# Seven seven-product pairs instead of eight in the gated MLP's up projection, with three plain pairs at its end

## The chip, the cores and the metric

The kernel runs on one NeuronCore of a Trainium2 chip. The core has five engines that work beside each other, each through its own instructions in order: TensorE (PE in the profile; its weight loads are PEld), VectorE (DVE), ScalarE (ACT), GpSimd (POOL) and SyncE (SP, which here only issues transfers). ACT issues transfers too (ACTq in the rows). The metric is the device time of one execution in microseconds (us): the median of three runs before is 1050.01 us (1048.56 to 1051.01).

## The reference, cut to what matters

One layer of an encoder over 512 tokens of width 1024 in float32: four token mixers, a cross-attention into 256 memory tokens, and a gated MLP with a causal depthwise convolution. The change lies in the MLP:

```python
hf = _rms_norm(x, norm_ffn_pre[l])
u = _dwconv_causal(hf @ w_up[l], ffn_dw[l]) + ffn_dw_b[l]      # 1024 -> 2 x 2816, width 3
u_g, u_v = jnp.split(u, 2, axis=-1)
yff = (jax.nn.silu(u_g) * u_v) @ w_down[l]                     # 2816 -> 1024
x = x + _rms_norm(yff, norm_ffn_post[l])
```

## The kernel before, in words

**Numbers.** A float32 matrix is held as two parts: a high part (a cast on ACT, `wh`, `hth`, `tokh`) and a low part (the value less its high part, on DVE, `wl`, `htl`, `tokl`). A product is three matmuls: high by high, and each high by the other's low (`mm3`, which ends in L244).

**Up projection (`up_jobs`).** The 5632 columns of `w_up` are 22 gate blocks and 22 value blocks of 128 columns; pair j is gate block j with value block j. A block's result is channels by tokens (128 x 512) in a PSUM bank, summed over 8 row tiles. A *plain* block takes 8 x 3 matmuls with 512 moving columns (`plain`, `channel_major`), so a plain pair takes 48. A *seven-product* pair (`seven`) takes both blocks as a 2 x 2 matrix (upper and lower half of the 1024 rows, gate and value) by a 2 x 2 matrix of `hf` (upper and lower half of the channels, first and second 256 tokens), and does seven products instead of eight in Winograd's form: 7 x 4 x 3 = 84 matmuls with 256 moving columns. It needs sums of its weights (four GpSimd additions in `load_a`, on the raw tiles `wq`, into `sums` and `s`), three additions of products (on DVE, with the copies `mu` on ACT), and four sums of tokens, which all seven-product pairs share: `token_sums` builds them in the last four `qa` tiles, and `token_split` splits them into `tokh` and `tokl`. Of a pair that is done, `done` adds the bias, convolves (`taps`, L624), and leaves silu(gate) times value in half of a `qa` tile; `qa` tile q holds pairs 2q and 2q + 1.

Before, pairs 0 to 4 are plain, then eight times a seven-product pair (5, 7, ... 19) is interleaved with the plain pair behind it (6, 8, ... 20), and pair 21 is plain.

**Down projection (`down_jobs`).** It runs Winograd's form over token halves, column halves of `w_down` and the two pairs in a `qa` tile, in two phases over q = 0 to 10. Phase 0 makes products M1, M6, M5, M7 into all eight PSUM banks. Its weights come in two tiles `dw` for each q, of parts of `w_down` and of weight sums that went through DRAM: class `Sums` loads two tiles `wp` (ACT queue, L568), adds (L572 to L575) and stores (L579), one q at a time, in the loop over the up pairs. The buffers of `wp` serve the third and fourth `dw` tile later, the two of `wq` the first and second. The activations of q must be summed first: `down_sums(q)`, three GpSimd additions of 128 x 256 (L1665 to L1667), the last of which writes into the `qa` tile. Room for the sums (`down_places`): the tile `z7` for q = 0 and 1, `tokh` for q = 2 to 9 and `tokl` for q = 10, which come free only when the last seven-product pair has read them. `activations(phase, q)` then splits `qa` and `pairs`: for q = 0 into the two `wr` tiles, for q = 1 to 4 into quarters of the tiles of `hf` (`hth`, `htl`), which come free when the last up block has been multiplied.

**Order.** `run_blocks` fetches the weights of three jobs ahead of the one it multiplies. The program is then put in order by a scheduler that goes by a modelled time, within the dependences; `issue_after` adds an order against one instruction. The order on each engine is fixed in the program, and each engine takes its instructions strictly in turn.

Of the kernel before, what the change touches and what calls it, by code (L numbers as in the profile page):

```python
# [25 lines left out]
P = 128  # L26
# [3 lines left out]
NK = D // P  # L30
# [56 lines left out]
def hybrid_layer(ctx: ExitStack, tc: tile.TileContext, a: dict, out: bass.AP):  # L87
# [1109 lines left out]
    def then(f):  # L1197

        return None, None, f
# [447 lines left out]

    def token_split(i):
        hi, lo = ns.tok
        split_to(hi[:, i], lo[:, i], ns.quart[i - 4])  # L1650

    def split_to(hi, lo, x):
        A.copy(hi, x)  # L1653
        V.tensor_tensor(lo, x, hi.bitcast(F32), ALU.subtract)  # L1654
# [14 lines left out]
    def up_jobs():  # L1669
# [27 lines left out]
        def plain(j, i, then=None):  # L1697
            def body(hi, lo):
                ps = bank()
                channel_major(ps, (hi, lo), ns.hf)  # L1700
                done(j, i, ps)
                if then:
                    then()
            return *block(j, i), body
# [31 lines left out]
                        sums_step(f, x, "taps")  # L1736
            return now

        yield plain(2, 0, steps(("store", 0)))
        yield plain(2, 1, steps(("load", 1), ("split", 1)))  # L1740
        yield plain(3, 0, steps(("add", 1), ("split", 0)))
        yield plain(3, 1, steps(("store", 1), ("split", 2)))
        yield plain(4, 0, steps(("load", 2), ("split", 3)))
        yield plain(4, 1, steps(("add", 2)))

        def seven(j):

            z = SimpleNamespace()

            def load_a():  # L1750
                z.g, z.v = [load_block(j, i) for i in range(2)]
                w = split_weights(z.g, [P, NK, P], shift=HALF_SHIFT)
                z.s = ns.fp.tile([P, D], F32, tag="z7", name="sums2")
                a11, a12, a21, a22 = (x[:, c] for x in (z.g, z.v) for c in (slice(0, S), slice(S, D)))
                s1, s2 = z.s[:, :S], z.s[:, S:]
                G.tensor_tensor(s1, a21, a22, ALU.add)
                G.tensor_tensor(s2, s1, a11, ALU.subtract)
                G.tensor_tensor(a21, a11, a21, ALU.subtract)
                z.t = ns.fp.tile([P, S], F32, tag="th", name="s4")
                G.tensor_tensor(z.t, a12, s2, ALU.subtract)  # L1760
                return w

            def load_block(j, i):
                raw = dw_tile("wq", 2, 2)
                SP.dma_start(raw.rearrange("p (k c) -> p k c", k=NK), block(j, i)[0])
                return raw

            def product(ps, w, k0, x, start):
                for k in range(4):
                    mm3(ps, w[0][:, k0 + k], w[1][:, k0 + k], x[0](k), x[1](k), start and k == 0, k == 3, True)  # L1770

            def part(k0, t):
                return [lambda k, h=h: h[:, k0 + k, (first, second)[t]] for h in ns.hf]

            def summed(i):
                return [lambda k, h=h: h[:, i, k] for h in ns.tok]

            def body_a(*w):
                z.r1, z.r2 = bank("sc"), bank("tr")
                z.m = ns.fp.tile([P, 2, HALF], F32, tag="mu", name="mu")  # L1780
                product(z.r2[:, first], w, 0, part(0, 0), True)
                A.copy(z.m[:, 0], z.r2[:, first])
                product(z.r1[:, first], w, 4, part(4, 0), True)
                V.tensor_tensor(z.r1[:, first], z.r1[:, first], z.m[:, 0], ALU.add)

            def body_b(*w):
                product(z.r2[:, first], w, 4, summed(1), False)
                A.copy(z.m[:, 1], z.r2[:, first])
# [17 lines left out]
            return (load_a, body_a, (lambda: split_weights(z.s, [P, NK, P], shift=HALF_SHIFT), None, body_b),  # L1806
                    (lambda: split_weights(z.v, [P, NK, P], shift=HALF_SHIFT), None, body_c),
                    (lambda: split_weights(z.t, [P, 4, P], shift=HALF_SHIFT), None, body_d), then(end))

        for q, j in enumerate(range(5, NF - 2, 2)):  # L1810
            load_a, body_a, b, c, d, e = seven(j)
            a = load_a, None, body_a
            tail = {}

            def first_half(hi, lo, tail=tail):
                tail.update(ps=bank(), w=(hi, lo))
                for k in range(4):
                    mm3(tail["ps"], hi[:, k], lo[:, k], ns.hf[0][:, k], ns.hf[1][:, k], k == 0, False)

            def second_half(j, tail=tail):  # L1820
# [5 lines left out]
            end = j + 4 > NF  # L1826
            yield a
            yield plain(j + 1, 0)
            yield then(lambda q=q: sums_step("store", q + 2, "first"))
            yield b  # L1830
            if end:
                yield then(lambda q=q: sums_step("load", q + 3, "taps"))
            yield (*block(j + 1, 1), first_half)
            if end:
                ns.pair_sums = []
                yield then(lambda: (down_places(("z7", 2)), down_sums(0, 1)))
            else:
                yield then(lambda q=q: sums_step("load", q + 3, "taps"))
            yield c
            yield d  # L1840
            yield then(lambda j=j, f=second_half: f(j + 1))
            if end:
                yield then(lambda q=q: add_sums(q + 3, V, "taps"))
# [238 lines left out]
```

## Time and profile before

| | |
|---|---|
| median of the runs | 1050.01 us |
| the profiled execution | 1049.59 us |
| its span in the trace | 1047.7 us |
| granted TensorE clock, mean over the span | 0.993 |
| busy: PE, DVE, ACT, POOL | 1024.8, 855.1, 534.0, 290.7 us |

The profiled execution is 1.9 us longer than its span, and 0.4 us below the median. In the rows, "out<-in" names the tile that is written and those that are read, "ps_mm", "ps_av", "ps_sc" and "ps_tr" are PSUM banks, and "[x <-E tile L]" is the engine's idle time before an instruction with what ended it. The MLP begins at about 690 us; the up projection ends and the down projection begins at 923 us.

### The profile page before, as it was taken

What the parts mean: (1) busy time and instruction counts of PE and PEld (TensorE: products, weight loads), DVE (VectorE), ACT (ScalarE), POOL (GpSimd) and SP (SyncE); (2) the same over time, 40 slices, a digit from 0 to 9 for tenths busy, and PEclk for the clock granted to TensorE, in tenths of its full rate; (3) what the DMA queues carried; (4) which work ended last, traced back from release to release, by engine and by line L of the source; (5) the groups of instructions that cost most, each with busy time, mean ns of one, the idle gap of its engine ahead of it and who ended that gap; (6) DMA issues with size and microseconds to landing.
All of it is one profiled execution on the core that took longest, in us unless ns stands there. A gap on an engine that the chain in (4) does not pass through costs nothing.

```text
span 1047.7 us, 15194 instructions
## 1 busy us (share of the span) xinstructions
PE 1024.8 (98%) x5477; PEld 883.3 (84%) x5477; DVE 855.1 (82%) x1290; ACT 534.0 (51%) x893; POOL 290.7 (28%) x303
## 2 busy tenths in 40 slices
PE   9999999999999999999999999999999999969997
PEld 7888888888888988888888899898789899848885
DVE  7899998677788668878677898769887887879786
ACT  5322222376565465765535666554455454545662
POOL 4001000100020224332000030166077547696001
PEclk9999999999999999999999999999999999989999
DMA  7954333334444356676368743054776566536562
GB/s 252 307 171 106 101 101 101 91 91 127 135 116 114 94 136 180 173 195 172 122 206 266 222 141 121 22 181 127 235 241 200 182 220 204 180 120 221 195 209 90
DMA packets 194129, 169.41 MB, mean 162 GB/s; under 512 B 25295, under 2 KB 165692, under 8 KB 194053
## 3 DMA queue, kind: packets, MB, share of 16 engines
q1 hardware_dynamic: 185011, 136.69, 44.1%
q10 hardware_dynamic: 6482, 23.21, 6.0%
q0 software_dynamic: 2560, 8.54, 2.6%
q8 instruction: 43, 0.70, 0.3%
q14 instruction: 33, 0.27, 0.1%
HBM read 142.18 MB, written 26.23 MB: 161 GB/s over the span
## 4 chain that ended last, share of the span: by engine, by line
PE 87%; DMA 4%; DVE 4%; POOL 2%; issue 2%; ACT 2%; ACTq 0%; SPq 0%; POOLq 0%; DVEq 0%
PE ps_mm L244 38%; PE ps_av L244 23%; PE ps_tr L244 14%; PE ps_sc L244 9%; PE ps_tr L250 1%; DMA dw<-sums 1%; POOL pairs L1666 1%; DMA sums<-wp 1%; DVE wl L202 1%; DMA ptl<-turned 1%; DMA e<-in_w_in 1%; POOL pairs L1665 1%; PE ps_mm L462 1%; DMA wp<-in_w_down 1%; PE ps_av L462 1%
## 5 line engine op out<-in xcount | busy, mean ns | idle before, releaser
L201 ACT CAST wh<-wr 128x1024 fp32r<-128x1024 f32 (+1 forms) x124 | 129.4, 1046 | 185.6 <-PE ps_mm L244 67.7
L202 DVE TENSOR_TENSOR wl<-wr,wh 128x1024 fp32r<-128x1024 f32 (+1 forms) x124 | 161.9, 1307 | 37.5 <-ACT wh L201 36.9
L244 PE MATMUL ps_mm<-htl,wh 128*128 128x512 f32 (+1 forms) x472 | 173.5, 376 | 0.0
L244 PE MATMUL ps_mm<-hth,wh 128*128 128x512 f32 (+1 forms) x472 | 173.5, 376 | 0.0
L244 PE MATMUL ps_mm<-hth,wl 128*128 128x512 f32 (+1 forms) x472 | 173.2, 375 | 0.0
L244 PEld LDWEIGHTS ps_mm<-hth,wl 128*128 128x128 f32 x472 | 87.0, 188 | 15.8
L244 PEld LDWEIGHTS ps_mm<-hth,wh 128*128 128x128 f32 x472 | 87.0, 188 | 15.3 <-ACT hth L164 0.3
L244 PEld LDWEIGHTS ps_mm<-htl,wh 128*128 128x128 f32 x472 | 87.0, 188 | 15.3
L244 PE MATMUL ps_av<-htl,wh 128*128 128x512 f32 (+1 forms) x264 | 97.7, 370 | 0.0
L244 PE MATMUL ps_av<-hth,wh 128*128 128x512 f32 (+1 forms) x264 | 97.6, 370 | 0.0
L244 PE MATMUL ps_av<-hth,wl 128*128 128x512 f32 (+1 forms) x264 | 97.6, 370 | 0.0
L697 DVE SCALAR_TENSOR_TENSOR y<-y,par,y 128x508 f32<-128x508 f32 (+29 forms) x120 | 82.5, 726 | 0.1
L244 PEld LDWEIGHTS ps_av<-htl,wh 128*128 128x128 f32 x264 | 49.6, 188 | 8.2
L244 PEld LDWEIGHTS ps_av<-hth,wl 128*128 128x128 f32 x264 | 49.6, 188 | 8.0
L244 PEld LDWEIGHTS ps_av<-hth,wh 128*128 128x128 f32 x264 | 49.7, 188 | 7.9
L1654 DVE TENSOR_TENSOR wl<-dw,wh 128x1024 fp32r<-128x1024 f32 x32 | 44.0, 1377 | 7.7 <-ACT wh L1653 7.5
L1653 ACT CAST wh<-dw 128x1024 fp32r<-128x1024 f32 x32 | 33.5, 1050 | 17.8 <-PE ps_tr L244 5.7
L244 PE MATMUL ps_tr<-htl,wh 128*128 128x512 f32 (+1 forms) x112 | 40.6, 363 | 0.0
L244 PE MATMUL ps_tr<-hth,wh 128*128 128x512 f32 (+1 forms) x112 | 40.6, 363 | 0.0
L244 PE MATMUL ps_tr<-hth,wl 128*128 128x512 f32 (+1 forms) x112 | 40.4, 360 | 0.0
L1124 POOL TENSOR_SCALAR fbias<-ck,cq 128x128 f32<-128x128 f32 (+3 forms) x32 | 21.3, 670 | 66.2 <-DVE st L1130 61.1
L811 POOL MEMSET qk<- 64x512 f32 x16 | 8.5, 532 | 90.5 <-PE ps_sc L244 31.8
(558 smaller groups left out, 2770.8 us busy)
## 6 DMA issues: line engine op xcount, KB each, us to landing
wr<-in_w_in SPq DMA_DIRECT2D x38, 512.0 KB
wr<-in_w_gate SPq DMA_DIRECT2D x32, 512.0 KB
wr<-in_w_up SPq DMA_DIRECT2D x28, 512.0 KB
wp<-in_w_down ACTq DMA_DIRECT2D x22, 512.0 KB
sums<-wp ACTq DMA_DIRECT2D x22, 512.0 KB
dw<-sums SPq DMA_DIRECT2D x44, 256.0 KB
wr<-in_w_branch SPq DMA_DIRECT2D x16, 512.0 KB
wq<-in_w_up SPq DMA_DIRECT2D x16, 512.0 KB
```

What stands on the lines that cost most here:

```text
L201: last_weights[:] = [order(A.copy(hi, raw[:, :n])).ins, low.tensor_tensor(lo, raw[:, :n], hi.bitcast(F32), ALU.subtract).ins]
L202: low.tensor_tensor(lo, raw[:, :n], hi.bitcast(F32), ALU.subtract).ins]
L244: steps_of[:] = [PE.matmul(ps, lhs, rhs, start=start, stop=stop, skip_group_check=again).ins]
L250: turns.append(PE.transpose(ps, x, ident[:n, :n]).ins)
L462: keep(PE.matmul(banks[c][:, :S // 2], w[p == 1][:, k, c * P:(c + 1) * P], ht[p == 2][:, i * 4 + k, :S // 2], start=(i, p, k) == (0, 0, 0) ...
L697: ins = V.scalar_tensor_tensor(dst[:, s:], src[:, :S - s], pc("conv_dw", k * 4 + j), dst[:, s:], ALU.mult, ALU.add)
L811: G.memset(qk[rows[1 - c], 4 + c].bitcast(F32), 0.0)
L1124: G.tensor_scalar(bias[:, :w], ck[j][:, :w], -1.0, cq[:, qt, head:head + 1], ALU.mult, ALU.add)
L1653: A.copy(hi, x)
L1654: V.tensor_tensor(lo, x, hi.bitcast(F32), ALU.subtract)
L1665: G.tensor_tensor(t[:, 0], x[:, 1], x[:, 3], ALU.add)
L1666: G.tensor_tensor(t[:, 1], x[:, 0], x[:, 1], ALU.subtract)
```

## The change

The loop over seven-product pairs stops one earlier: pairs 5, 7, ... 17 are seven-product (seven of them), each with the plain pair behind it, and pairs 19, 20 and 21 are plain, six plain blocks in a row. The last rounds of `Sums` and all of `down_sums` beyond q = 0 and 1 are spread over these blocks. The additions of q = 2 in `Sums` go from DVE to GpSimd, which makes those of q = 3 to 9 in both kernels; those of q = 0, 1 and 10 stay on DVE. `token_split` makes its low part on GpSimd instead of DVE. The two raw tiles of pair 5 are asked for two blocks sooner in the job list.

```diff
     def token_split(i):
         hi, lo = ns.tok
-        split_to(hi[:, i], lo[:, i], ns.quart[i - 4])
+        A.copy(hi[:, i], ns.quart[i - 4])
+        G.tensor_tensor(lo[:, i], ns.quart[i - 4], hi.bitcast(F32)[:, i], ALU.subtract)
...
+            def load_raws():
+                z.g, z.v = [load_block(j, i) for i in range(2)]
+
             def load_a():
-                z.g, z.v = [load_block(j, i) for i in range(2)]
+                if not hasattr(z, "g"):
+                    load_raws()
...
-        for q, j in enumerate(range(5, NF - 2, 2)):
-            load_a, body_a, b, c, d, e = seven(j)
+        pairs = {j: seven(j) for j in range(5, NF - 4, 2)}
+        yield plain(2, 0, steps(("store", 0)))
+        yield plain(2, 1, steps(("load", 1), ("split", 1)))
+        yield plain(3, 0, steps(("add", 1), ("split", 0)))
+        yield then(pairs[5][0])
+        yield plain(3, 1, steps(("store", 1), ("split", 2)))
+        yield plain(4, 0, steps(("load", 2), ("split", 3)))
+        yield plain(4, 1, lambda: add_sums(2, G, "taps"))
+
+        for q, j in enumerate(pairs, 2):
+            _, load_a, body_a, b, c, d, e = pairs[j]
...
             yield e
-            if not end:
-                yield then(lambda q=q: ns.sums.add(q + 3, G))
-        yield then(lambda: down_places(("tokh", 8), ("tokl", 1)))
-        yield plain(NF - 1, 0, lambda: (sums_step("store", NF // 2 - 1, "taps"), down_sums(2, 3)))
-        yield plain(NF - 1, 1, lambda: down_sums(*range(4, NF // 2)))
+            yield then(lambda q=q: ns.sums.add(q + 1, G))
+        ns.pair_sums = []
+        last = NF // 2 - 1
+        yield then(lambda: (down_places(("z7", 2), ("tokh", 8), ("tokl", 1)), down_sums(0, 1)))
+        yield plain(NF - 3, 0, lambda: (sums_step("store", last - 1, "taps"), sums_step("load", last, "taps")))
+        yield plain(NF - 3, 1, lambda: down_sums(2, 3))
+        yield plain(NF - 2, 0, lambda: (add_sums(last, V, "taps"), down_sums(4, 5)))
+        yield plain(NF - 2, 1, lambda: down_sums(6, 7))
+        yield plain(NF - 1, 0, lambda: (sums_step("store", last, "taps"), down_sums(8, 9)))
+        yield plain(NF - 1, 1, lambda: down_sums(10))
```

How the built order moves is shown at three places. The numbers behind a name tell tiles apart: `qa_6860` to `qa_6870` are the `qa` tiles of q = 0 to 10.

ACT, where the down projection begins, before: `htl_8945` and `hth_8944` are the split activations, `wh_9084` the high weights of q = 2, `wh_8994` and `wh_9057` those of q = 1.

```order
L1653 CAST hth_8944<-qa_6861 128x512
L1653 CAST hth_8944<-pairs_8839 128x512
L1678 ACTIVATE c_8979<-ps_av_8998,par2_406 128x512
L1653 CAST hth_8944<-pairs_8939 128x512
L1653 CAST htl_8945<-pairs_8939 128x512
L579 DMA sums_6875<-wp_8817 128x1024
L1653 CAST hth_8944<-qa_6862 128x512
L1681 ACTIVATE c_8979<-c_8979 128x512
L1653 CAST htl_8945<-qa_6863 128x512
L1653 CAST wh_9084<-dw_8991 128x1024
L1653 CAST htl_8945<-qa_6864 128x512
L1653 CAST wh_8994<-dw_8871 128x1024
```

ACT at the same place in the changed kernel, where `wh_8955` and `wh_9000` are the high weights of q = 1, `c_8940` belongs to pair 21, and `wp_8757` to the last weight sums.

```order
L579 DMA sums_6875<-wp_8757 128x1024
L1679 ACTIVATE c_8940<-ps_mm_8915,par2_406 128x512
L1682 ACTIVATE c_8940<-c_8940 128x512
L1654 CAST wh_8955<-dw_8853 128x1024
L1654 CAST wh_9000<-dw_8902 128x1024
L1654 CAST htl_8906<-qa_6863 128x512
L1654 CAST htl_8906<-pairs_8711 128x512
L1654 CAST htl_8906<-qa_6864 128x512
L1654 CAST hth_8905<-qa_6861 128x512
L1654 CAST hth_8905<-pairs_8710 128x512
L1679 ACTIVATE c_8940<-ps_av_8959,par2_406 128x512
L1654 CAST hth_8905<-qa_6862 128x512
```

The weights of q = 1, which stood behind the casts of `qa_6862`, `qa_6863` and `qa_6864`, now stand ahead of them.

POOL, the additions of the last weight sums that it makes and the first of `down_sums`, before: `pairs_8839` lies in `z7`, `pairs_8939` in `tokh`.

```order
L574 TENSOR_TENSOR wp_8634<-wp_8635,wp_8634 128x512
L575 TENSOR_TENSOR wp_8635<-wp_8635,wp_8634 128x512
L1665 TENSOR_TENSOR pairs_8839<-qa_6860 128x256
L1666 TENSOR_TENSOR pairs_8839<-qa_6860 128x256
L1665 TENSOR_TENSOR pairs_8839<-qa_6861 128x256
L1666 TENSOR_TENSOR pairs_8839<-qa_6861 128x256
L1667 TENSOR_TENSOR qa_6860<-pairs_8839,qa_6860 128x256
L1667 TENSOR_TENSOR qa_6861<-pairs_8839,qa_6861 128x256
L1665 TENSOR_TENSOR pairs_8939<-qa_6862 128x256
```

POOL in the changed kernel, from the additions of q = 9 on; `pairs_8711` lies in `tokh`.

```order
L572 TENSOR_TENSOR wp_8627<-wp_8627,wp_8626 128x512
L573 TENSOR_TENSOR wp_8626<-wp_8626 128x512
L574 TENSOR_TENSOR wp_8626<-wp_8627,wp_8626 128x512
L575 TENSOR_TENSOR wp_8627<-wp_8627,wp_8626 128x512
L1666 TENSOR_TENSOR pairs_8711<-qa_6862 128x256
L1667 TENSOR_TENSOR pairs_8711<-qa_6862 128x256
L1666 TENSOR_TENSOR pairs_8711<-qa_6863 128x256
```

The sums of q = 0 and 1 now stand ahead of the last weight sums on POOL, and those of q = 2 to 9 right behind these. In both orders `qa_6862`, `qa_6863` and `qa_6864` are written late: before by the 16th, 18th and 19th addition counted from the first into `tokh`, now by the 14th, 15th and 17th.

DVE at the same place, before, from the last tap of pair 21 on: `wl_8995` and `wl_9058` are the low weights of q = 1.

```order
L624 SCALAR_TENSOR_TENSOR c_8979<-ps_av_8998,par0_398,c_8979 128x511
L1654 TENSOR_TENSOR wl_9085<-dw_8991,wh_9084 128x1024
L1654 TENSOR_TENSOR htl_8945<-qa_6864,htl_8945 128x512
L1654 TENSOR_TENSOR wl_8995<-dw_8871,wh_8994 128x1024
L1683 TENSOR_TENSOR qa_6870<-c_8979 128x512
L1654 TENSOR_TENSOR wl_9058<-dw_8941,wh_9057 128x1024
```

DVE in the changed kernel, from the second low weight tile of q = 1 on; `wl_9028` belongs to q = 2.

```order
L1655 TENSOR_TENSOR wl_9001<-dw_8902,wh_9000 128x1024
L1655 TENSOR_TENSOR htl_8906<-qa_6863,htl_8906 128x512
L1655 TENSOR_TENSOR htl_8906<-pairs_8711,htl_8906 128x512
L1655 TENSOR_TENSOR htl_8906<-qa_6864,htl_8906 128x512
L1655 TENSOR_TENSOR hth_8905<-qa_6861,hth_8905 128x512
L1655 TENSOR_TENSOR hth_8905<-pairs_8710,hth_8905 128x512
L624 SCALAR_TENSOR_TENSOR c_8940<-ps_av_8959,par0_398,c_8940 128x510
L1655 TENSOR_TENSOR hth_8905<-qa_6862,hth_8905 128x512
L1655 TENSOR_TENSOR hth_8905<-pairs_8711,hth_8905 128x512
L1655 TENSOR_TENSOR htl_8906<-pairs_8711,htl_8906 128x512
L624 SCALAR_TENSOR_TENSOR c_8940<-ps_av_8959,par0_398,c_8940 128x511
L1655 TENSOR_TENSOR wl_9028<-dw_8952,wh_9027 128x1024
```

The two taps of the last block, which free its PSUM bank, now stand among the splits of the activations of q = 1 to 4, and the low weights of q = 1 ahead of them.

SP's queue takes the first raw tiles of pair 5 at the same place as before: behind the first six blocks of `w_up`.

More of the change, by code (lines that the diff above doesn't have):

```diff
@@ L1737, in steps @@
             return now
[L1739 to L1744, printed above, removed]
         def seven(j):
             z = SimpleNamespace()
+            def load_raws():
+                z.g, z.v = [load_block(j, i) for i in range(2)]
             def load_a():
-                z.g, z.v = [load_block(j, i) for i in range(2)]
+                if not hasattr(z, "g"):
+                    load_raws()
                 w = split_weights(z.g, [P, NK, P], shift=HALF_SHIFT)
@@ L1824, in second_half @@
                 done(j, 1, tail["ps"])
-            end = j + 4 > NF
             yield a
             yield plain(j + 1, 0)
-            yield then(lambda q=q: sums_step("store", q + 2, "first"))
+            yield then(lambda q=q: sums_step("store", q, "first"))
             yield b
-            if end:
-                yield then(lambda q=q: sums_step("load", q + 3, "taps"))
             yield (*block(j + 1, 1), first_half)
[L1834 to L1838, printed above, removed]
+            yield then(lambda q=q: sums_step("load", q + 1, "taps"))
             yield c
```

4 lines of the change are left out of this document (1 added, 3 removed).

## The prediction

> **What bounds the kernel now.** I read the page first, then who TensorE waits for, then windows around the waits.
>
> ```profile
> PE 1024.8 (98%) x5477; PEld 883.3 (84%) x5477; DVE 855.1 (82%) x1290; ACT 534.0 (51%) x893; POOL 290.7 (28%) x303
> ```
>
> TensorE is busy 98% of the span, so a gain is either fewer matmuls or fewer waits of TensorE. Its waits, longest first:
>
> ```profile
> PE ps_sc L244 <- ACT wh L1653: 10.0, 1, 10.0
> PE ps_tr L244 <- ACT mu L1782: 1.5, 1, 1.5
> PE ps_tr L244 <- ACT mu L1788: 1.4, 1, 1.4
> ```
>
> The columns are total, times, longest. The first lies where the up projection gives way to the down projection, the other two in the first seven-product pair. The windows give start:end, length, busy time of PE, PEld, DVE, ACT, POOL, then the granted clock:
>
> ```profile
> 710.30:742.90 32.60, 32.60 (x146) 27.01 (x145) 31.43 (x32) 16.36 (x20) 14.69 (x7) 1.00 0.51 162
> 762.00:923.20 161.20, 161.20 (x1007) 145.37 (x1006) 131.04 (x152) 81.66 (x116) 107.58 (x68) 1.00 0.61 196
> 928.30:938.40 10.10, 0.05 (x2) 0.05 (x1) 4.62 (x6) 4.29 (x7) 10.10 (x13) 0.64 0.26 87
> 938.40:942.00 3.60, 3.60 (x10) 2.89 (x11) 3.60 (x3) 1.21 (x2) 3.60 (x3) 0.59 0.42 141
> 942.00:995.00 53.00, 53.00 (x236) 43.86 (x235) 45.73 (x43) 32.52 (x41) 19.52 (x15) 1.00 0.62 203
> ```
>
> From 762 to 923 us, and from 942 on, TensorE never stops. Between 928.3 and 938.4 it stands, GpSimd alone works through, and the clock is granted at 0.64, and 0.59 in the next 3.6 us. What TensorE waits for there:
>
> ```profile
> 923.80 0.61 ACT L1653 CAST hth<-qa 128x512 fp32r<-128x512 f32 x1
> 924.33 0.62 ACT L1653 CAST hth<-pairs 128x512 fp32r<-128x512 f32 x1
> ...
> 933.90 0.62 ACT L1653 CAST hth<-qa 128x512 fp32r<-128x512 f32 x1 [7.25 <-POOL qa L1667]
> 937.26 1.99 ACT L1653 CAST wh<-dw 128x1024 fp32r<-128x1024 f32 x2
> ...
> 914.40 0.75 POOL L1665 TENSOR_TENSOR pairs<-qa 128x256 f32<-128x256 f32 x1 [9.27 <-PE ps_tr L244]
> 923.58 2.50 POOL L1666 TENSOR_TENSOR pairs<-qa 128x256 f32<-128x256 f32 x1
> 929.75 0.71 POOL L1665 TENSOR_TENSOR pairs<-qa 128x256 f32<-128x256 f32 x1
> 933.15 0.71 POOL L1667 TENSOR_TENSOR qa<-pairs,qa 128x256 f32<-128x256 f32 x1
> ```
>
> POOL can begin the sums into `tokh` only at 914.40, when the last seven-product pair is through. The first that ACT may split is written at 933.15, while ACT stands for 7.25 us with the weights of q = 1 queued behind that cast. The place's limit is the late start of POOL's sums.
>
> **The products.** Chain pieces give the pace of matmuls:
>
> ```profile
> 890.28 2.83 PE ps_tr L244 x24
> 896.82 4.99 PE ps_mm L244 x22
> ```
>
> One matmul of 512 columns takes 4.99/22 = 0.227 us, one of 256 takes 2.83/24 = 0.118. A plain pair is 48 x 0.227 = 10.9 us, a seven-product pair 84 x 0.118 = 9.9. Turning pair 19 plain adds **1.0 us**. What goes with it (four additions on POOL, one and a half weight splits and three additions on DVE, three copies on ACT) I cost at nothing, since TensorE is busy throughout 762 to 923. That a run of plain blocks keeps pace shows in 710.3 to 742.9: six blocks, no wait, beside token sums and weight sums.
>
> **The wait at the down projection.** The e product of pair 17 is the first half of the piece at 890.28, so it ends at 891.7, and `tokh` is free then. Six plain blocks of 24 x 0.227 = 5.45 us follow; the up projection ends at E = 891.7 + 32.7 = 924.4. In the new order POOL has the weight sums of q = 9 ahead:
>
> ```profile
> 891.25 1.30 POOL L572 TENSOR_TENSOR wp<-wp 128x512 f32<-128x512 f32 x1 [1.93 <-DMA wp<-in_w_down]
> 897.32 1.29 POOL L575 TENSOR_TENSOR wp<-wp 128x512 f32<-128x512 f32 x1
> ...
> L1666 POOL TENSOR_TENSOR pairs<-qa 128x256 f32<-128x256 f32 x9 | 12.1, 1351 | 0.0
> L1665 POOL TENSOR_TENSOR pairs<-qa 128x256 f32<-128x256 f32 x8 | 9.6, 1198 | 9.3 <-PE ps_tr L244 9.3
> L1667 POOL TENSOR_TENSOR qa<-pairs,qa 128x256 f32<-128x256 f32 x7 | 7.7, 1120 | 0.0
> ```
>
> These additions end at 898.6; their load set their start, so I keep them there. ACT's store of these sums waits for them, and behind it stands the weight cast of pair 20's first block, which TensorE needs at 891.7 + 2 x 5.45 = 902.6: some 3 us to spare for a cast of 1.0. ACT, whose weight casts of q = 1 now stand ahead, then needs `qa` of q = 4, the 17th addition from there. By the means of 914 to 945 us (1.35, 1.20, 1.12; over 24 instructions 1.23) it is written at 898.6 + 20.9 = 919.5; by the ten before 929.75, the slowest stretch ((929.75 - 914.40)/10 = 1.53), at 924.6. ACT comes to that cast at E + 2.2 = 926.6 (a weight cast, half of the 1.99 at 937.26, and casts 0.53 us apart, as at 923.80 and 924.33), so it doesn't wait either way. The wait of **10.05 us** goes, and the slow clock behind it:
>
> ```profile
> 938.35 1.22 PE ps_sc L244 x2
> 939.57 0.85 PE ps_tr L244 x2
> 940.42 1.18 PE ps_av L244 x3
> ```
>
> Seven matmuls in 3.25 us, where seven at 0.227 are 1.59: **1.7 us** more.
>
> What is late next: q = 0 gives TensorE 21 matmuls (E + 4.8), then it needs the first activations and weights of q = 1. ACT has one weight cast and five casts to do behind E: 1.0 + 5 x 0.53 + 0.1 = E + 3.8, in time by 1.0. Then DVE: behind E + 1.1 come a low weight tile, five splits, a tap, three splits, and the tap that frees the second `ps_av` bank, which TensorE reaches after 46 matmuls, E + 10.4.
>
> ```profile
> 928.53 0.68 DVE L1654 TENSOR_TENSOR htl<-pairs,htl 128x512 fp32r<-128x512 f32 x1
> 934.55 1.23 DVE L1654 TENSOR_TENSOR hth<-qa,hth 128x512 fp32r<-128x512 f32 x1 [5.35 <-ACT hth L1653]
> 936.84 0.74 DVE L624 SCALAR_TENSOR_TENSOR c<-ps_av,par,c 128x511 f32<-128x511 f32 x1
> 937.50 1.77 DVE L1654 TENSOR_TENSOR wl<-dw,wh 128x1024 fp32r<-128x1024 f32 x1
> L1654 DVE TENSOR_TENSOR tokl<-qa,tokh x4: 1210/1213/3411, 722.7 to 735.7; 128x1024 fp32r<-128x1024 f32 x4
> ```
>
> At the short times (1.21, 0.68, 0.74) that is 8.1 us and ends at E + 9.2, no wait; at the long ones (1.77, 1.23, 0.74) 13.1 us, E + 14.2, a wait of 3.8. POOL still works then and both lengths occur beside it, so I take the middle: **1.9 us** comes back, of 0 to 3.8.
>
> **The start of the seven-product pairs.** DVE loses the four `tokl` splits (1.21 + 1.21 + 1.21 + 3.41 = 7.0 us) and the weight sums of q = 2 (four instructions of 128 x 512, as the 0.68 row: 2.7). POOL gains both, and has room:
>
> ```profile
> 718.89 6.18 POOL L1646 TENSOR_TENSOR qa<-qa 128x1024 f32<-128x1024 f32 x2
> 760.26 1.30 POOL L1756 TENSOR_TENSOR sums<-wq 128x512 f32<-128x512 f32 x1 [35.19 <-DMA wq<-in_w_up]
> ...
> 754.18 0.79 ACT L1678 ACTIVATE c<-ps_mm,par 128x512 f32<-128x512 f32 x1
> 759.59 0.37 ACT L1788 COPY mu<-ps_tr 128x256 f32<-128x256 f32 x1 [4.62 <-DVE wp L575]
> ```
>
> Four splits at 6.18/2 = 3.1 us and the weight sums at 898.6 - 891.25 = 7.4 are 19.8 us in 35.19 us of idle time. One behind the other they end at 725.1 + 12.4 = 737.5; TensorE needs `tokl` only behind pair 5's first 24 matmuls and a plain block, 742.9 + 2.8 + 5.4 = 751.1. The two waits for `mu` (1.5 and 1.4) come from ACT, which stood for 4.62 us behind a store of weight sums that DVE made late. With DVE some 4 us ahead, the first wait should go. The second depends on POOL's sums of q = 2: their load is about 4 us earlier, but four additions take 7.4 us there against 2.7, so that wait stays or grows by a little. Bounds: both go (-2.9), or none does and a little is added (+0.5). I take **-1.7**. The raw tiles of pair 5 cost and bring nothing: SP takes them at the same place in its queue.
>
> **The sum**, against the profiled execution: 1049.6 + 1.0 - 10.05 - 1.7 + 1.9 - 1.7 = 1039.05 us. The profiled execution is 0.4 below the median of the runs shown, so against the median I forecast **1039.4 us**. With the ends of the terms: 1036.3 (no wait comes back, both `mu` waits go) to 1043.5 (3.8 comes back, +0.5 at the start).
>
> [...]
>
> **Rivals.**
>
> *The weights of q = 1 come late.*
>
> ```profile
> 884.45 0.34 ACTq L568 DMA_DIRECT2D wp<-in_w_down  x1
> 923.36 0.33 ACTq L579 DMA_DIRECT2D sums<-wp  x1
> 926.10 0.33 SPq L591 DMA_DIRECT2D dw<-in_w_down  x1
> ```
>
> They go into the buffers of the last `wp`, so they need its load, DVE's additions, the store and the load of `dw`, one behind the other; ACT's casts behind E are queued behind them. For it: a load takes 6.8 us to the additions (884.45 to 891.25). Against it: the store stands on ACT behind block (20, 1), which ends at E - 10.9, a weight cast (1.0) and an evacuation (0.79, the row at 754.18), so at about E - 9; its `dw` follows 2.7 us later before (923.36 to 926.10), so `dw` is asked for at about E - 6, and the chain can be 6 us late before the cast, due at E, is held up. If the chain is 12 us late, TensorE waits 6 and pays the slow clock: 1039.4 - 1.9 + 6 + 1.7 = 1045.2 us.
>
> *GpSimd's token splits hold up DVE.*
>
> ```profile
> 738.05 1.21 DVE L202 TENSOR_TENSOR wl<-wq,wh 128x1024 fp32r<-128x1024 f32 x1
> ```
>
> In 710.3 to 742.9 DVE has 1.2 us to spare and is relieved of 9.7. If each of the 19.8 us on POOL held up an instruction of DVE for its whole length, DVE would be 8.9 us late, and the weights of pair 5, whose low part is done at 739.3 for 742.9, would cost TensorE 8.9 - 3.6 = 5.3 us: 1039.4 + 1.7 + 5.3 = 1046.4. For it speaks the 3411 among the four `tokl`, beside a POOL instruction; against it that the three others took 1.21. [...]
>
> *Slower: POOL becomes the bound.* If the 17 additions take m each, the cast of q = 4 waits from m = (926.6 - 898.6)/17 = 1.65 us on. Without any wait there the sum is 1037.5 against the median; to be slower than 1052.1 it takes 14.6 us, of which the slow clock is 1.7: 12.9 us of waiting, m = (28.0 + 12.9)/17 = 2.4 us. At 2.5 it gives 1053.7. One row of 24 is that long (2.50 at 923.58, beside a busy DVE); the mean is 1.23.
>
> *No change.* If the cast of `qa` came as far behind E as before (933.90 against 923.2), TensorE would wait as before: 1050.0 + 1.0 - 1.7 = 1049.3. The sums' start 15.8 us earlier (898.6 against 914.40) excludes it nearly.
>
> **How the numbers follow.** Likeliest 68% (1036.3 to 1043.5), late weights 12%, held-up DVE 7%, slower 6%, no change 2%; 5% lie below. The range reaches down a little below the likeliest and up over the late weights, and leaves out the slower end, no change and most of what lies below: 1035.5 to 1046.0. Below 0.2% (2.1 us, about what a measurement of this kernel can tell from no change) on either side count as same: faster 92%, same 2%, slower 6%.
>
> **What would show it.** Right: no wait of TensorE over 4 us near 924 us and a clock of 1.00 there; POOL's last sum for q = 4 written before ACT's cast; the up projection's end within 2 us of 923; at most one `mu` wait. Wrong: ACT or TensorE waiting for `dw` or for `qa` behind E, or the low weights of pair 5 done later than 739.3.

## The result, and the profile after

The changed kernel takes 1051.23 us (median of 20 runs, 1049.13 to 1054.29), the kernel before 1049.2 us in 20 runs beside it (1047.3 to 1051.95). The ratio is 1.0019, with a 95% interval of 1.001 to 1.0027: a little slower, where 1039.4 us, 1% faster, was forecast. The first line of the page after, and who TensorE waits for after (total, times, longest):

```profile
PE 1027.1 (98%) x5441; PEld 883.2 (84%) x5441; DVE 856.3 (82%) x1277; ACT 532.1 (51%) x888; POOL 299.4 (29%) x307
```

```profile
PE ps_sc L244 <- ACT hth L1654: 4.5, 1, 4.5
PE ps_tr L244 <- ACT mu L1780: 2.7, 1, 2.7
PE ps_mm L244 <- DVE c L624: 2.4, 1, 2.4
PE ps_mm L244 <- DVE wl L202: 1.7, 1, 1.7
...
PE ps_sc L244 <- DVE ps_sc L1782: 0.7, 1, 0.7
```

The wait of 10 us is gone, but five smaller ones stand in its place. Only the first of them lies at the down projection; the other four (2.4 + 1.7 + 2.7 + 0.7 = 7.5 us) lie at the first seven-product pair, where two waits of 2.9 us in all stood before.

To see where the time went, the same stretches of matmuls are set side by side: from the first block of pair 2 to the last product of the first seven-product pair, on to the end of the up projection, the next 130 matmuls, and the rest. The windows of before:

```profile
710.50:765.60 55.10, 52.26 (x264) 44.05 (x263) 50.33 (x55) 26.48 (x35) 19.75 (x11) 1.00 0.59 197
765.60:923.25 157.65, 157.65 (x985) 142.19 (x985) 128.37 (x149) 79.40 (x113) 104.03 (x66) 1.00 0.60 195
923.25:964.60 41.35, 31.30 (x131) 25.39 (x130) 35.71 (x34) 22.04 (x30) 36.80 (x30) 0.88 0.53 176
964.60:1047.70 83.10, 75.90 (x345) 62.82 (x343) 64.55 (x79) 43.49 (x65) 7.62 (x15) 0.98 0.51 169
```

The same of after:

```profile
709.80:770.45 60.65, 53.11 (x264) 43.95 (x263) 52.10 (x48) 26.32 (x35) 35.82 (x18) 1.00 0.54 176
770.45:929.03 158.58, 158.58 (x949) 141.36 (x948) 131.95 (x144) 77.44 (x109) 116.33 (x80) 1.00 0.61 199
929.03:965.98 36.95, 32.49 (x132) 26.14 (x130) 32.04 (x34) 21.86 (x30) 14.63 (x13) 0.91 0.58 189
965.98:1048.40 82.42, 75.56 (x345) 62.90 (x343) 64.03 (x78) 43.73 (x66) 9.88 (x15) 0.99 0.51 167
```

The start lost 5.55 us, the six plain blocks cost 0.93 us, the down projection's beginning gained 4.40 us, and the rest 0.68 us; what lies ahead of these stretches was 0.70 us shorter in this execution. Together that is +0.7 us, which is what the spans say (1048.4 against 1047.7). The medians lie 2.0 us apart, and some 0.6 us of that stands outside the span: each of the 20 runs of the changed kernel takes 2.4 to 2.7 us more than its span, each run of the kernel before 1.8 to 1.9, and each run below that has the token splits on DVE alone 1.75 to 2.15. Why that is stays open. Two things are to be explained: the 5.55 us at the start, and why the beginning of the down projection gained 4.4 us and not 10.

**The start.** DVE's timeline of after, beside GpSimd's:

```profile
717.18 0.73 DVE L624 SCALAR_TENSOR_TENSOR c<-ps_sc,par,c 128x510 f32<-128x510 f32 x1
...
722.23 2.88 DVE L1684 TENSOR_TENSOR qa<-c 128x512 f32<-128x512 f32 x1
725.03 2.88 DVE L573 TENSOR_TENSOR wp<-wp 128x512 f32<-128x512 f32 x1
727.83 3.41 DVE L202 TENSOR_TENSOR wl<-wr,wh 128x1024 fp32r<-128x1024 f32 x1
731.16 0.68 DVE L574 TENSOR_TENSOR wp<-wp 128x512 f32<-128x512 f32 x1
731.76 0.73 DVE L624 SCALAR_TENSOR_TENSOR c<-ps_mm,par,c 128x510 f32<-128x510 f32 x1
```

```profile
716.65 2.87 POOL L1651 TENSOR_TENSOR tokl<-qa,tokh 128x1024 fp32r<-128x1024 f32 x1
...
721.72 2.83 POOL L1646 TENSOR_TENSOR qa<-qa 128x1024 f32<-128x1024 f32 x1
724.52 2.83 POOL L1651 TENSOR_TENSOR tokl<-qa,tokh 128x1024 fp32r<-128x1024 f32 x1
727.32 2.84 POOL L1646 TENSOR_TENSOR qa<-qa 128x1024 f32<-128x1024 f32 x1
```

In these rows the two engines take turns: GpSimd's instructions end at 724.55, 727.35 and 730.16, DVE's next ones behind them at 725.11, 727.91 and 731.24, each 0.6 to 1.1 us after. An addition of 128 x 512 on DVE that takes 0.68 us when GpSimd is idle (731.16) takes 2.88 beside it: its own time and 2.2 us more, most of the 2.4 us that a GpSimd instruction of 128 x 1024 takes while DVE is idle (2.39 at 700.50). A tap, which reads PSUM, keeps its 0.73 us beside GpSimd (717.18). DVE's taps, queued behind these instructions, free the bank late (the 2.4 us), and the weight sums of q = 0, their store and the load of q = 1 on ACT's queue slip, which makes the three waits behind it.

**The down projection.** The last weight sums on DVE, their store and the first weight cast of q = 1 on ACT, and the load of `dw` between them on SP:

```profile
921.60 1.18 DVE L572 TENSOR_TENSOR wp<-wp 128x512 f32<-128x512 f32 x1
...
925.11 1.11 DVE L575 TENSOR_TENSOR wp<-wp 128x512 f32<-128x512 f32 x1
```

```profile
928.97 0.33 SPq L591 DMA_DIRECT2D dw<-in_w_down  x1
```

```profile
925.11 1.48 ACTq L579 DMA_DIRECT2D sums<-wp  x2
926.63 0.78 ACT L1679 ACTIVATE c<-ps_mm,par 128x512 f32<-128x512 f32 x1 [2.60 <-DVE wp L575]
...
934.10 1.04 ACT L1654 CAST wh<-dw 128x1024 fp32r<-128x1024 f32 x1 [1.48 <-DMA dw<-sums]
935.38 1.04 ACT L1654 CAST wh<-dw 128x1024 fp32r<-128x1024 f32 x1 [0.24 <-DMA dw<-sums]
...
937.89 0.61 ACT L1654 CAST hth<-qa 128x512 fp32r<-128x512 f32 x1
```

The up projection ends at 929.03. The last weight sum is made only 2.8 us ahead of that, with ACT standing 2.60 us for it; its store goes out at 926.25, `dw` is asked for at 928.97, 2.7 us behind the store, ACT waits for it, and the activations of q = 1 are cast behind the weights, at 937.89, where TensorE has been waiting since 934.1. GpSimd is no longer in this chain, but its 24 activation sums run from 902 to 930 us, and DVE's additions of 128 x 512 take 1.11 to 1.18 us beside them.

### The profile page after: what moved, and what is told of

Its sections match the earlier page's. It is cut to its first block, busy times and chain, and to the rows that moved or that the text cites. A ratio compares the mean times of both kernels' runs of the same rounds, so it can differ in the third digit from the quotient of the medians.

```text
span 1048.4 us, 15100 instructions
## 1 busy us (share of the span) xinstructions
PE 1027.1 (98%) x5441; PEld 883.2 (84%) x5441; DVE 856.3 (82%) x1277; ACT 532.1 (51%) x888; POOL 299.4 (29%) x307
## 4 chain that ended last, share of the span: by engine, by line
PE 86%; DVE 4%; POOL 4%; DMA 3%; issue 2%; ACT 1%; SPq 0%; ACTq 0%; POOLq 0%; DVEq 0%
PE ps_mm L244 38%; PE ps_av L244 22%; PE ps_tr L244 14%; PE ps_sc L244 10%; DVE wl L202 1%; PE ps_tr L250 1%; DMA sums<-wp 1%; DMA wp<-in_w_down 1%; POOL pairs L1666 1%; POOL pairs L1667 1%; DVE c L624 1%; POOL qa L1668 1%; PE ps_mm L462 1%; PE ps_av L462 1%; DMA dw<-sums 0%
## 5 line engine op out<-in xcount | busy, mean ns | idle before, releaser
L201 ACT CAST wh<-wr 128x1024 fp32r<-128x1024 f32 (+1 forms) x126 | 131.5, 1047 | 200.9 <-PE ps_mm L244 57.5
L202 DVE TENSOR_TENSOR wl<-wr,wh 128x1024 fp32r<-128x1024 f32 (+1 forms) x126 | 170.6, 1355 | 40.9 <-ACT wh L201 40.5
L244 PE MATMUL ps_mm<-hth,wh 128*128 128x512 f32 (+1 forms) x480 | 176.7, 376 | 2.4 <-DVE c L624 2.4
L244 PE MATMUL ps_mm<-hth,wl 128*128 128x512 f32 (+1 forms) x480 | 176.4, 376 | 1.7 <-DVE wl L202 1.7
L244 PE MATMUL ps_mm<-htl,wh 128*128 128x512 f32 (+1 forms) x480 | 176.6, 376 | 0.0
L244 PE MATMUL ps_av<-htl,wh 128*128 128x512 f32 (+1 forms) x272 | 100.8, 371 | 0.0
L244 PE MATMUL ps_av<-hth,wh 128*128 128x512 f32 (+1 forms) x272 | 100.7, 370 | 0.0
L244 PE MATMUL ps_av<-hth,wl 128*128 128x512 f32 (+1 forms) x272 | 100.7, 370 | 0.0
```

The source lines that it names most:

```text
L201: last_weights[:] = [order(A.copy(hi, raw[:, :n])).ins, low.tensor_tensor(lo, raw[:, :n], hi.bitcast(F32), ALU.subtract).ins]
L202: low.tensor_tensor(lo, raw[:, :n], hi.bitcast(F32), ALU.subtract).ins]
L244: steps_of[:] = [PE.matmul(ps, lhs, rhs, start=start, stop=stop, skip_group_check=again).ins]
```

## The experiments

The lengths of the first three stretches, by the same marks as in the windows above, and the times (all in us; the ratio is to the kernel before on the same chip):

| kernel | start | up to the end of the up projection | next 130 matmuls | median | ratio, 95% interval |
|---|---|---|---|---|---|
| before | 55.10 | 157.65 | 41.35 | 1049.2 | 1 |
| after | 60.65 | 158.58 | 36.95 | 1051.23 | 1.0019 (1.001 to 1.0027) |
| both moves to GpSimd at the start undone | 54.75 | 158.58 | 36.58 | 1043.94 | 0.9958 (0.9945 to 0.9972) |
| the same, again | 55.40 | 158.57 | 36.83 | 1044.26 | 0.996 (0.9947 to 0.9972) |
| only the weight sums of q = 2 on DVE | 60.72 | 158.56 | 37.23 | 1051.55 | 1.0021 (1.001 to 1.0032) |
| only the token splits on DVE | 55.87 | 158.57 | 35.66 | 1046.58 | 0.9979 (0.9968 to 0.9991) |
| both undone, GpSimd kept busy | 61.84 | 158.58 | 37.79 | 1052.36 | 1.0033 (1.0018 to 1.0047) |
| before with the token splits on GpSimd | 60.85 | 157.64 | 41.34 | 1054.53 | 1.0053 (1.0039 to 1.0068) |
| last weight sums a block earlier | 61.28 | 158.56 | 36.43 | 1051.12 | 1.0024 (1.0015 to 1.0032) |
| both undone, sums of q = 5 to 9 late | 54.85 | 158.56 | 37.78 | 1046.37 | 0.9974 (0.9962 to 0.9985) |
| both undone, sums of q = 7 to 9 late | 55.06 | 158.57 | 37.09 | 1045.41 | 0.9966 (0.9953 to 0.9978) |
| the same, last weight sums earlier | 54.59 | 158.57 | 37.89 | 1045.59 | 0.9966 (0.9953 to 0.9978) |
| both undone, sums of q = 5 to 9 left out | 54.89 | 158.57 | 31.57 | 1040.13 | 0.9918 (0.9901 to 0.9934) |

**Both moves to GpSimd at the start undone.**

```diff
-        G.tensor_tensor(lo[:, i], ns.quart[i - 4], hi.bitcast(F32)[:, i], ALU.subtract)
+        V.tensor_tensor(lo[:, i], ns.quart[i - 4], hi.bitcast(F32)[:, i], ALU.subtract)
...
-        yield plain(4, 1, lambda: add_sums(2, G, "taps"))
+        yield plain(4, 1, lambda: add_sums(2, V, "taps"))
```

> The changed kernel with the low parts of the token sums and the weight sums of q = 2 back on DVE; the end of the up projection stays as changed. Theory A (GpSimd's work beside DVE at the first seven-product pair costs what was lost there, 5.5 us): TensorE's waits between 728 and 762 us fall from 7.4 us to the 2.9 of before, and the time to about 1046 us, 3 us under the kernel before. Rival (the loss comes from another place, for example from the six plain blocks or from pair 5's raw tiles): about 1051 us, as the changed kernel.

1043.94 us: 7.3 us below the changed kernel, more than expected, and faster than the kernel before by 0.42%. The start takes 54.75 us, as before. So the loss lies in these two lines, and not in the plain blocks or the raw tiles of pair 5 (without the call that asks for them sooner, the built order of instructions is the same on all five engines, so that part of the change does nothing). Beside two of the runs below it gave 1044.26:

> The kernel with both edits at the start undone once more, on the chip of the two runs above, to compare them with it: 1043 to 1045 us, ratio to before 0.995 to 0.997.

**Each move alone.** The first run puts only the second line of that diff back on DVE, the second only the first.

> The changed kernel with only the weight sums of q = 2 back on DVE, the token splits' low parts still on GpSimd. Theory A (the token splits alone hold DVE up): the waits of 2.4 and 1.7 us near 734 and 750 us stay, the time within 1 us of the changed kernel, 1050 to 1052 us. Rival (the 7.1 us that GpSimd takes for these sums delay ACT's store, and `mu` behind it): 3 to 5 us faster, 1046 to 1048 us.

> The changed kernel with only the token splits' low parts back on DVE; the weight sums of q = 2 stay on GpSimd. Theory A (the token splits alone make the loss at the start): 1043 to 1045 us, as with both undone. Rival (each of the two moves costs by itself, the second where the first is not there to hide it): 1046 to 1049 us.

With the splits on GpSimd, the place of the weight sums of q = 2 makes no difference (1.0021 against 1.0019). With the splits on DVE, the sums on GpSimd cost something: 0.9979 against 0.9958 and 0.996. In the trace `mu` waits 2.6 us behind their store instead of 1.4. How much it is stays open: 0.5 to 1.1 us in the start's length, 0.9 less in the next stretch, and some 2 us in the times; the execution traced here is the fastest of its eight (1044.51 against a median of 1046.58). The splits make the loss; theory A stands, with the rival right in its second half.

**GpSimd kept busy for nobody.** To tell whether the loss comes from GpSimd's work as such or from a late result, both lines are on DVE and GpSimd makes the same subtractions into a tile that is overwritten later:

```diff
+        V.tensor_tensor(lo[:, i], ns.quart[i - 4], hi.bitcast(F32)[:, i], ALU.subtract)
+        G.tensor_tensor(ns.quart[5], ns.quart[i - 4], hi.bitcast(F32)[:, i], ALU.subtract)
```

> As the run with both edits undone at the start, with four GpSimd subtractions of 128 x 1024 more, beside the token splits, whose result nobody reads. Theory A (it is GpSimd's accesses that stretch DVE's instructions, whoever needs the result): DVE's two-operand instructions near 725 to 740 us take 2 to 3 us instead of 0.7 to 1.2, TensorE waits 3 to 6 us more than in the run without them, 1049 to 1052 us. Rival (what costs is that the low parts come late, or the order on ACT): as the run without them, about 1046 us, with DVE's instructions at their short times.

1052.36 us: the whole loss is back. DVE's timeline without GpSimd's four instructions, and then with them:

```profile
733.54 2.35 DVE L1651 TENSOR_TENSOR tokl<-qa,tokh 128x1024 fp32r<-128x1024 f32 x2
735.80 0.68 DVE L1684 TENSOR_TENSOR qa<-c 128x512 f32<-128x512 f32 x1
...
737.07 1.21 DVE L202 TENSOR_TENSOR wl<-wq,wh 128x1024 fp32r<-128x1024 f32 x1
```

```profile
733.49 6.09 DVE L1651 TENSOR_TENSOR tokl<-qa,tokh 128x1024 fp32r<-128x1024 f32 x2
739.51 2.88 DVE L1685 TENSOR_TENSOR qa<-c 128x512 f32<-128x512 f32 x1
742.31 0.74 DVE L624 SCALAR_TENSOR_TENSOR c<-ps_mm,par,c 128x510 f32<-128x510 f32 x1
742.97 2.70 DVE L202 TENSOR_TENSOR wl<-wq,wh 128x1024 fp32r<-128x1024 f32 x1
```

```profile
731.88 12.71 POOL L1652 TENSOR_TENSOR qa<-qa,tokh 128x1024 f32<-128x1024 f32 x4 [7.84 <-ACT tokh L1650]
```

DVE does the same instructions in the same order, and up to 733.5 us at the same times. From there on, beside GpSimd, four of them take 11.67 us instead of 4.24: 7.4 us more. The low weights of pair 5 are late, and TensorE waits for them as the prediction's rival had it:

```profile
PE ps_tr L244 <- DVE wl L202: 3.5, 1, 3.5
```

**One part of the change alone.** The kernel before, with `token_split` as in the change:

> The kernel before with one part of the change: the token splits' low parts on GpSimd. Theory A: TensorE's waits near 733, 750 and 755 us appear as in the changed kernel, some 5 to 7 us, all of them ahead of the last wait, which stays at 10 us: 1054 to 1057 us. Rival (the loss needs the changed kernel's other moves): 1049 to 1051 us.

1054.53 us, 0.53% slower than before: the start takes 60.85 us instead of 55.10 (waits of 2.4 and 2.7 us, and 3.4 us of slow clock, with 0.94 granted over this stretch, where before it had waits of 2.9 us at 1.00), the stretches behind it are as long as before. Of the last one the composition differs from what was expected, a wait of 5.6 us and two smaller ones instead of one of 10, but not the length (41.34). That one line is worth +5.7 us by itself.

**The last weight sums a block earlier.** The changed kernel with

```diff
-        yield plain(NF - 3, 1, lambda: down_sums(2, 3))
-        yield plain(NF - 2, 0, lambda: (add_sums(last, V, "taps"), down_sums(4, 5)))
+        yield plain(NF - 3, 1, lambda: (add_sums(last, V, "taps"), down_sums(2, 3)))
+        yield plain(NF - 2, 0, lambda: (sums_step("store", last, "taps"), down_sums(4, 5)))
...
-        yield plain(NF - 1, 0, lambda: (sums_step("store", last, "taps"), down_sums(8, 9)))
+        yield plain(NF - 1, 0, lambda: down_sums(8, 9))
```

> The changed kernel with the last weight sums (q = 10) one block earlier on DVE and their store one block earlier on ACT, the start as changed. Theory B (the wait at the down projection comes from the last sums being added late, so that ACT waits for `dw` with the casts behind it): `dw` of q = 1 lands some 5 us earlier, the 4.5 us wait and most of the slow clock's 2.7 us go, 1044.5 to 1047 us. Rival (ACT's two weight casts and seven activation casts behind the end of the up projection set that wait, whenever `dw` lands): the wait shrinks by no more than the 1.7 us for which ACT waited on `dw`, 1049 to 1051 us.

1051.12 us, no gain, so this way of bringing `dw` forward failed. The additions start 8 us earlier on DVE, but stand among other work there and take 1.20 to 1.26 us each, and the last ends 3.6 us ahead of the up projection's end instead of 2.8. ACT, whose store now stands earlier in its queue, waits for it with its casts and evacuations behind:

```profile
926.03 1.05 ACT L1654 CAST wh<-dw 128x1024 fp32r<-128x1024 f32 x1 [10.17 <-DVE wp L575]
```

The 4.5 us wait shrinks to 1.0, and one of 2.6 us for a tap's bank comes in its place. This points to DVE's time as the bound rather than to the place of the additions, so the next runs took GpSimd's work away from beside DVE instead.

**GpSimd's activation sums moved behind the end of the up projection**, from the run with both lines undone, first those of q = 5 to 9, then those of q = 7 to 9 alone, then these with the last weight sums a block earlier as well. The edit of the first:

```diff
-        yield plain(NF - 2, 0, lambda: (add_sums(last, V, "taps"), down_sums(4, 5)))
-        yield plain(NF - 2, 1, lambda: down_sums(6, 7))
-        yield plain(NF - 1, 0, lambda: (sums_step("store", last, "taps"), down_sums(8, 9)))
+        yield plain(NF - 2, 0, lambda: (add_sums(last, V, "taps"), down_sums(4)))
+        yield plain(NF - 2, 1)
+        yield plain(NF - 1, 0, lambda: sums_step("store", last, "taps"))
...
-                    G.tensor_tensor(z[:, 1], z[:, 2], z[:, 1], ALU.subtract)
+                    ns.fold = G.tensor_tensor(z[:, 1], z[:, 2], z[:, 1], ALU.subtract).ins
+            if (phase, q) == (0, 3):
+                with tc.issue_after(ns.fold):
+                    down_sums(5, 6, 7, 8, 9)
```

> As the run with the token splits' low parts and the weight sums of q = 2 back on DVE, and beyond that GpSimd's activation sums of q = 5 to 9 (15 additions) put behind the start of the down projection; the order on DVE and ACT up to there is unchanged. Theory C (the wait at the down projection has the same cause as the loss at the start: GpSimd's additions beside the last six plain blocks stretch DVE's instructions, so the last weight sums, their store and `dw` of q = 1 come late): the last weight sum on DVE, 2.5 us ahead of the up projection's end in that run, ends some 4 us sooner, the 5.1 us wait falls to 1 or 2 us, 1040 to 1042 us. Rival (ACT's casts behind the end of the up projection set the wait, or `dw` is held by SP's queue): the wait stays over 4 us, 1043 to 1045 us. Against both: the sums of q = 5 come too late and a new wait appears 25 us behind.

> As the run with both edits at the start undone, with GpSimd's activation sums of q = 7 to 9 only (9 additions) put behind the start of the down projection; the instruction order on DVE, ACT and SP is that of the run it is compared with. Theory C: the last weight sums on DVE start when GpSimd is through, so they end some 4 us sooner and the 5.1 us wait falls to about 1 us, as with five sums moved; the sums of q = 5 and 6 are in time, so the waits near 957 us (3 us) don't come back: 1041 to 1043 us, 1 to 3 us below that run. Rival (whatever GpSimd adds beside DVE is paid once, wherever it stands): 1044 to 1046 us.

> As the run with the sums of q = 7 to 9 late, and the last weight sums one block earlier on DVE and ACT. Theory C: with the stretching gone an earlier place helps, since `dw` of q = 1 then lands ahead of the up projection's end: 0.5 to 2 us faster than that run, 1040 to 1042 us. Rival: the additions stand among GpSimd's sums again and are stretched, or ACT's evacuations come behind a wait for `dw`, as in the run that moved them alone: equal or up to 2 us slower.

None is faster than the run with both lines undone: 1046.37, 1045.41 and 1045.59 us against 1044.26 (by the ratios, 0.9974, 0.9966 and 0.9966 against 0.996; the last two are not clear of it). The first step goes as theory C has it. With five sums late, DVE's timeline reads

```profile
913.96 0.68 DVE L572 TENSOR_TENSOR wp<-wp 128x512 f32<-128x512 f32 x1
...
916.13 0.69 DVE L575 TENSOR_TENSOR wp<-wp 128x512 f32<-128x512 f32 x1
```

at the short times, 6.3 us ahead of the up projection's end (2.5 in the run it comes from), and the waits of TensorE there are

```profile
PE ps_sc L244 <- DVE wl L1655: 2.1, 1, 2.1
PE ps_av L244 <- DVE c L624: 2.1, 1, 2.1
...
PE ps_sc L244 <- ACT hth L1654: 1.3, 1, 1.3
```

The wait for `hth` fell from 5.1 to 1.3 us, and matmul 24 of the down projection starts 4.4 us sooner. But the sums stand beside DVE's splits now, which take 1.22 and 1.75 us there instead of 0.68 and 1.21, ACT waits 5 us for the first of the late sums, and the new waits for `wl` and for a tap give it all back. With three sums late the first wait is 3.1 us (about 1 was expected) and the other two 0.6 and 0.2; the stretch is 37.09 us against 36.83. Theory C's price was wrong: moved work is not saved work.

**The same sums left out.** The kernel leaves out GpSimd's 15 additions for q = 5 to 9 and splits parts of the activations in place of the sums, so its result is of other numbers. The order on DVE, ACT and SP is that of the run with both lines undone.

```diff
...
+            ns.pair_sums[5:10] = [ns.quart[q][:, 2:] for q in range(5, 10)]
...
-        yield plain(NF - 2, 1, lambda: down_sums(6, 7))
+        yield plain(NF - 2, 1)
...
```

> As the run with both edits at the start undone, but GpSimd's activation sums of q = 5 to 9 (15 additions) are left out: the down projection splits parts of the activations themselves in their place, so these five products are of other numbers. The order on DVE, ACT and SP is unchanged. Theory C (those additions cost DVE time wherever they stand, ahead of the up projection's end or behind it): without them the first wait at the down projection is about 1 us, as with the five sums moved, and no wait of 2 us follows near 957 us; some 4 us below that run, 1039 to 1041 us. Rival (the first wait has another cause and the later one belongs to late sums alone): 1042 to 1044 us.

1040.13 us, 4 us below the run with the sums, in the range expected. The 130 matmuls behind the up projection take 31.57 us instead of 36.58, with a granted clock of 1.00 instead of 0.95, and the waits there are nearly gone:

```profile
PE ps_av L244 <- DVE c L624: 1.0, 1, 1.0
PE ps_sc L244 <- ACT hth L1654: 0.4, 1, 0.4
```

In the run with the sums no cast ahead of this wait waits for GpSimd, so it isn't a late sum that is saved. What is left of the wait at the down projection is the price of GpSimd's additions beside DVE: 15 of them cost 5 us in this stretch and 4 us in the time, and moving them behind the end of the up projection saved none of it. The chain of weights (sums, store, `dw`, cast) is how it reaches TensorE, not its cause.

## Why the prediction was wrong

- *A plain pair for a seven-product pair: +1.0 us.* Right; it is 0.93 us, and the stretch from pair 5 to the end of the up projection has no wait of TensorE, in any of the runs.
- *The 10.05 us wait and its slow clock go.* Half right. Its cause was named rightly: GpSimd's late start on the sums into `tokh`. After, 17 additions took 1.13 us each from 902.28 (1.23 was taken) and no cast waits for `qa`. But the rival "the weights of q = 1 come late", held at 12%, came in its place, with 4.5 us and 2.6 us of slow clock: in the window behind the wait, 5.29 us at a granted clock of 0.50, a matmul starts every 0.43 us (0.23 at 1.00), so half of the time is lost.

```profile
938.56:943.85 5.29, 5.29 (x13) 4.13 (x14) 5.29 (x8) 4.26 (x7) 3.92 (x4) 0.50 0.43 141
```

  The step that failed is the one against that rival: "the store stands on ACT behind block (20, 1) ... so at about E - 9", and so "`dw` is asked for at about E - 6". The store's place on ACT was counted, but DVE's time for the sums that it stores was put at nothing. DVE made the last of them at E - 2.8 (E is the end of the up projection), the store went out behind it, and `dw` was asked for at E itself, 2.7 us behind the store as the prediction had it.
- *1.9 us come back by the tap of the second bank.* Not in the changed kernel, where the longer wait hides it. With that wait shortened it appeared, with 2.1, 0.6, 0.5 and 1.0 us, inside the 0 to 3.8 given.
- *The start: -1.7 us, with bounds of -2.9 and +0.5.* Wrong, and the largest miss: +5.55 us. The step that failed is "With DVE some 4 us ahead, the first wait should go": the seven us of splits that DVE lost were more than made up by what GpSimd's splits did to the rest. The rival "GpSimd's token splits hold up DVE" has the mechanism and nearly the sum (7.0 us above the forecast; the stretch is 7.2 above it), though its wait for the low weights of pair 5 appears in that form only in the run with GpSimd kept busy: in the changed kernel these weights are done at 743.81, later than the 739.3 that the prediction named as a sign, but TensorE, held by the 2.4 us ahead, needs them only at 745.12. It got 7% on the ground that three of four `tokl` rows took 1.21 us. In the timeline of before:

```profile
722.75 3.41 DVE L1654 TENSOR_TENSOR tokl<-qa,tokh 128x1024 fp32r<-128x1024 f32 x1
...
729.68 1.21 DVE L1654 TENSOR_TENSOR tokl<-qa,tokh 128x1024 fp32r<-128x1024 f32 x1
...
734.52 2.35 DVE L1654 TENSOR_TENSOR tokl<-qa,tokh 128x1024 fp32r<-128x1024 f32 x2
```

  The three short ones begin at 729.68 and later, and GpSimd's token sums end at 718.89 + 6.18 = 725.1: they showed DVE without GpSimd beside it, and so spoke for nothing. The one row that stood beside GpSimd was the 3.41.
- *The chances.* Late weights and a held-up DVE were taken as alternatives with 12 and 7%. They have one kind of cause, GpSimd beside DVE, and came together: 1039.4 + 7.0 + 5.8 = 1052.2 by the prediction's own prices, against 1051.23. The measured sizes close the sum for the profiled execution: 1039.05 - 0.07 (the plain pair) + 5.45 (the down projection's beginning, where 9.85 was to be gained and 4.40 was) + 7.25 (the start) - 1.38 (the rest and what lies ahead) + 0.83 (outside the span) = 1051.13, against 1051.12. So the prices of the two rivals were near, and the last two terms, on which the prediction has nothing, cancel in part by luck. The case for a slower kernel was put on GpSimd's pace, which was as forecast.

## What to carry to other kernels

The work that went to an idle engine cost what it did to its neighbour (beside GpSimd four DVE instructions took 11.67 us instead of 4.24): before moving DVE work to GpSimd, sort DVE's rows by whether GpSimd ran beside them, and count the stretched time, not the mean. An instruction count that falls on DVE is no gain if each of the others grows by the length of GpSimd's; here four splits taken off DVE (7.0 us) cost 5.7 us net. A wait that is followed back to a chain of transfers may still be a matter of one busy engine at the chain's head: moving the chain's links changed nothing, taking away the contention did.

The best version found is the change without its two moves to GpSimd at the start: 0.9958 of the time before.

## What the runs showed of the hardware

In the rows above, DVE instructions with two operands in SBUF and GpSimd's instructions ran one behind the other (0.68 us against 2.88; two splits 2.35 against 6.09), while taps, which read PSUM, kept 0.73 to 0.74 us beside GpSimd.

The clock was less regular than expected. At the first of the waits at the start, TensorE stands 2.36 us in the changed kernel and 2.33 us in the run with the last weight sums earlier, at the same matmul; behind it the clock stays at 1.00 in the first and is granted at 0.50 in the second. What differs is where the wait lies. In the traces of before and after, the clock is granted at 0.50 for 10.24 us from 931.11 and for 6.83 us from 937.08, three and two times 3.41 us, and once more at the end of the span, from 1043.75 and from 1046.31: 112.64 and 109.23 us behind the first starts, 33 and 32 such steps. The steps around the wait, first of the run with the last weight sums earlier, then of the changed kernel, whose steps are laid back from 937.08:

```profile
731.02:734.43 3.41, 1.08 (x6) 0.86 (x6) 2.53 (x5) 1.35 (x2) 0.00 (x0) 1.00 0.63 171
734.43:737.84 3.41, 3.41 (x10) 2.64 (x9) 3.12 (x4) 0.89 (x2) 0.00 (x0) 0.50 0.89 329
```

```profile
728.87:732.28 3.41, 2.68 (x12) 1.88 (x10) 3.41 (x3) 0.00 (x0) 1.29 (x1) 1.00 0.00 0
732.28:735.69 3.41, 1.79 (x8) 1.52 (x9) 2.53 (x4) 2.13 (x3) 0.00 (x0) 1.00 0.87 279
735.69:739.11 3.42, 3.42 (x17) 2.84 (x16) 2.34 (x4) 0.11 (x1) 0.00 (x0) 1.00 0.85 262
```

In the one run the whole wait, 3.41 - 1.08 = 2.33 us, lies in one step, and the next step is slow; in the other it is split over two, 0.73 and 1.62 us, and none is. In the traces of before and after, four steps at 1.00 have a slow one behind them, and TensorE stood in them for 2.81 and 2.95 us (before, from 927.70 and 1040.34) and for 2.98 and 3.41 us (after, from 933.67 and 1042.90); the most that it stood in a step at 1.00 with another at 1.00 behind it is 1.46 us before (from 750.20) and 1.78 us after (from 756.18). In the slow step from 734.43 a matmul starts every 0.43 us instead of every 0.23, so about half of its length, 1.7 us, is lost. The prediction counted no slow clock for the 1.9 us that it let come back, or for the 3.8 at the end of its range; that was its author's estimate, and here a wait of 2.33 us brought one. Counted from the span's start, the steps lie differently in the two traces (931.11 and 937.08 are 5.97 us apart, not a whole number of steps), so of two runs with the same wait one can have a slow step behind it and the other not, as in the rows above. Two profiles of the same kernel lie 0.65 us apart at the start (54.75 and 55.40 us), where their two waits add up to 2.5 and 3.1 us.
